# RMSNorms of a two-block transformer kernel: row blocks in pairs, inverse roots by a power on GpSimd

## The chip, the cores and the metric

The kernel runs on one core of a Trainium2 chip. The core has a matmul engine (TensorE, PE in the profile), VectorE (DVE), ScalarE (ACT), GpSimd (POOL) and SyncE (SP, which here only issues transfers). Times are device microseconds (us) of one execution; the time of a kernel is the median of its runs.

## The reference

The input is a sequence of 512 tokens of width 1024. A first block mixes a gated delta rule (4 heads, chunks of 64, both directions, with a state that starts from a context of 256 tokens) and a banded attention of 8 heads; its result is added to x. The second block has two layers, each a feed-forward network, a mixer (causal latent attention beside a dilated one), a feed-forward network and a gated embedding. Each of these is wrapped in two norms: its output is normalised before it is added (postnorm), and the sum is normalised for the next one (prenorm).

```python
def rmsnorm(x, g):
    xf = x.astype(jnp.float32)
    y = xf * lax.rsqrt(jnp.mean(xf * xf, axis=-1, keepdims=True) + EPS)
    return (y * g.astype(jnp.float32)).astype(x.dtype)

def swiglu(x, w_gate, w_up, w_down):
    return (jax.nn.silu(x @ w_gate) * (x @ w_up)) @ w_down

# mixer: norms on the latents and on each group of heads
q = (rmsnorm(q_lat, q_norm) @ w_q_up)
kv = (rmsnorm(kv_lat, kv_norm) @ w_kv_up)
merged = jnp.concatenate([rmsnorm(o_mla, grp_gain[:MLA_WIDTH]),
                          rmsnorm(o_dil, grp_gain[MLA_WIDTH:])], axis=-1)
return merged @ w_out
```

All of it is in 32-bit floats.

## The kernel before

Activations lie with the 1024 features on the partitions, as 8 row blocks of 128, and the 512 tokens along the free axis. A matrix product is done in three passes, with each factor split in a high and a low part: ScalarE copies a weight into its high part wH (L78), VectorE subtracts to get wL (L80), or GpSimd does where the caller says `l="g"`; activations are split in the same way into xnH (L101) and xnL (L105). All matmuls of products come from L87.

A norm works on one half of the tokens (256 columns, `HALVES`). `SumSq.add` squares a row block on ScalarE (L156, L159) and adds it on VectorE into one accumulator (L160). `sums` (L133) multiplies the accumulator by a vector of ones, so that PE sums over the partitions: the result is one number for each token, as 128x2. `rsq` makes the inverse root of it on VectorE: scale and add (rq_v, L112), a first guess by integer shifts (L113, L114), three Newton rounds of three operations (L118 to L120), and where the norm has a factor of its own, a multiplication by it (rq_p, L124). `bcast` (L141) spreads the 256 numbers over all partitions by matmuls, into PSUM. Then `postnorm` scales each row block by gain and root (nt, L189), adds it into h (L191) and feeds the new h to the next SumSq; `prenorm` scales h (ny, L171, in `scaled_split`) and splits it. The tiles of these functions come from a pool `np_`: np1 in the first block (two buffers of each), np2 in the second (three).

Four stages follow each other in a layer: `ffn`, `mixer`, `ffn`, `ple`. The last products of a stage give its output one row block and half at a time, and the first products of the next stage wait for xnH and xnL of a half. In `mixer`, `group` is the norm over the four row blocks of a head group (om, od), and the latents have norms over two row blocks and one.

The first block ends with the delta-rule steps (`gdn_steps`, six steps of eight chains, 4 heads in two directions: a read of the state L598, a product with an inverse L605, the update L617, the output L628 and L629, whose temporaries are tiles gr_, vd and u) and window attention (`win_heads`: K, Q, V and a mask are loaded into a pool "wina", then scores psg<-wK,wQ, a masked softmax wS, transposes L1013, values L1021). The output of the delta rule is squared, normalised (osq) and transposed (L909).

Two things that the source does not spell out set the order. A scheduling layer places the instructions of each engine when the program is built, from the order of the code, the dependences and its own idea of durations. And pools lie on two stacks in SBUF, one from the left and one from the right; where a new tile takes bytes that an older one held, its first write waits for the last use of the older one.

Of the kernel before, what the change touches and what calls it, by code (L numbers as in the profile page):

```python
# [9 lines left out]
F32 = mybir.dt.float32  # L10
# [3 lines left out]
ALU = mybir.AluOpType  # L14
# [12 lines left out]
class Kern:  # L27
    def __init__(self, tc, ctx, I, O):
        self.tc, self.nc, self.I, self.O = tc, tc.nc, I, O
        self.n = 0  # L30
# [10 lines left out]
        nc.vector.memset(self.ones2, 1.0)  # L41

# [65 lines left out]
    def rsq(self, src, n, mul, add, post=None):  # L108

        nc, t = self.nc, lambda nm, dt=F32: self.np_.tile([128, 24], dt, name=nm, bufs=2)[:, :n]  # L110
        v, i, j = t("rq_v"), t("rq_i", I32), t("rq_j", I32)
# [33 lines left out]
    class SumSq:  # L145
        def __init__(self, K):
            self.K, self.a, self.n = K, [None, None], 0

        def add(self, src, scale=1.0):
            K, nc = self.K, self.K.nc  # L150
            p, n = src.shape[0], src.shape[-1]
            i = 0
            self.n += 1
# [12 lines left out]

    def scaled_split(self, H, L, src, gain, rsB, h="a", l="v"):

        n = src.shape[-1]
        y = self.np_.tile([128, 256], F32, name="ny", bufs=self.nb)[:, :n]  # L170
        self.nc.vector.scalar_tensor_tensor(y, src, gain, rsB, op0=ALU.mult, op1=ALU.mult)  # L171
        self.split(H, L, y, h, l)

    def prenorm(self, ss, c, gain):

        rsB = ss.rs(D, (c[1] - c[0]) // 128)
        for k in range(8):
            self.scaled_split(self.xnH[:, k, c[0]:c[1]], self.xnL[:, k, c[0]:c[1]], self.h[:, k, c[0]:c[1]],
                              gain[:, k:k + 1], rsB)

    def postnorm(self, ss, c, f, gain, post=None, out=None):
# [3 lines left out]
        s2 = self.SumSq(self) if out is None else None  # L185
        for k in range(8):
            t = self.np_.tile([128, 256], F32, name="nt", bufs=self.nb)[:, :c[1] - c[0]]
            hk = self.h[:, k, c[0]:c[1]]
            nc.vector.scalar_tensor_tensor(t, f[:, k, c[0]:c[1]], gain[:, k:k + 1], rsB, op0=ALU.mult, op1=ALU.mult)  # L189
# [3 lines left out]
            else:  # L193
                nc.vector.tensor_tensor(t, hk, t, op=ALU.add)
                nc.sync.dma_start(out[:, k, c[0]:c[1]], t)
# [649 lines left out]
    def merge_(self, ctx, wctx, hctx, heads):  # L845
# [94 lines left out]
        ss = [self.SumSq(self) for _ in HALVES]  # L940
# [95 lines left out]
    def ffn(self, l, j, g_out, g_next):  # L1036
# [3 lines left out]
        with ExitStack() as ctx:  # L1040
# [21 lines left out]
            ss = [self.SumSq(self) for _ in HALVES]  # L1062

            def down(W, part, dm, c):
# [14 lines left out]
                if part == len(PARTS) - 1:  # L1079
                    ss[0 if c[0] == 0 else 1].add(fk)  # L1080
# [103 lines left out]
    def mixer(self, l, G):  # L1184
# [8 lines left out]
        with ExitStack() as ctx:  # L1193
# [49 lines left out]
            with ExitStack() as c2:  # L1243
# [10 lines left out]
                for c in HALVES:  # L1254
                    n = c[1] - c[0]
                    sq, sk = self.SumSq(self), self.SumSq(self)
# [11 lines left out]
                    for z in range(3):  # L1268
                        self.scaled_split(latH[:, z, c[0]:c[1]], latL[:, z, c[0]:c[1]], lat[:, z, c[0]:c[1]], qn[:, z:z + 1],
                                          rq if z < 2 else rk)  # L1270
# [38 lines left out]
            def group(o, k0, halves=HALVES):  # L1309
                for c in halves:  # L1310
                    ss = self.SumSq(self)
                    for k in range(4):
                        ss.add(o[:, k, c[0]:c[1]])
                    rsB = ss.rs(512, 2)
                    for k in range(4):
# [389 lines left out]
```

## Time and profile before

| | |
|---|---|
| median of three runs | 3129.61 us (3122.44 to 3131.08) |
| profiled execution | 3144.24 us, of it 3142.3 us span |
| granted PE clock, mean | 0.944 of full speed |
| busy: PE, DVE, ACT, POOL | 2853.6, 1747.3, 1085.4, 344.7 us |

The span is the time from the first to the last instruction on the record. PE's busy share of 91% is an average: the first block has pauses in which PE waits for transfers, and the second has short ones around its norms. A wait belongs to the instruction that came last; the table of waits groups them by the waiting line and by what ended the wait.

### The profile page before, as it was taken

The page shows a single profiled execution, that of the slowest core. Times are in us where ns is not written, and L with a number is a line of the kernel's source. Part 1 is how long each engine was busy: PE and PEld are TensorE (multiplying, and loading weights), DVE is VectorE, ACT ScalarE, POOL GpSimd, SP SyncE. Part 2 cuts the span into 40 slices and gives each one's busy share as a digit, 9 for nine tenths or more (in the row PEclk, how much of TensorE's full clock was granted, in tenths as well). Part 3 has the DMA queues.
Part 4 walks back from the last instruction along what each step waited for, and adds up shares of the span by engine and source line. Part 5 has one row for each costly group of instructions (what it writes and reads, how often), then busy time and mean ns, then how long its engine had stood idle before and what let it go on. Part 6 is the DMA issues. An engine that isn't in the chain of part 4 may idle for free.

```text
span 3142.3 us, 41998 instructions
## 1 busy us (share of the span) xinstructions
PE 2853.6 (91%) x16048; PEld 2392.3 (76%) x16048; DVE 1747.3 (56%) x3733; ACT 1085.4 (35%) x2062; POOL 344.7 (11%) x199
## 2 busy tenths in 40 slices
PE   7999699999999997887999988999989787999987
PEld 2877588678888885667888878888887566888877
DVE  6678907666333475468523378423376457723357
ACT  3443225443222233563322234322233464322223
POOL 3023211422000011002000022000011001000010
PEclk8999769999999998998999998999999898999998
DMA  5325341443222136542222221322234643222321
GB/s 198 98 94 173 91 125 46 146 141 102 100 88 99 59 116 219 149 137 91 94 94 97 91 94 54 111 95 97 88 83 166 178 144 118 95 94 88 100 74 54
DMA packets 151584, 344.29 MB, mean 110 GB/s; under 512 B 37616, under 2 KB 58480, under 8 KB 150872
## 3 DMA queue, kind: packets, MB, share of 16 engines
q1 hardware_dynamic: 142168, 318.55, 31.9%
q10 hardware_dynamic: 9216, 23.07, 2.1%
q8 instruction: 126, 2.06, 0.3%
q14 instruction: 74, 0.61, 0.1%
HBM read 292.02 MB, written 49.54 MB: 109 GB/s over the span
## 4 chain that ended last, share of the span: by engine, by line
PE 71%; DVE 15%; ACT 4%; DMA 4%; issue 3%; POOL 2%; SPq 0%; ACTq 0%; DVEq 0%; POOLq 0%
PE psg L87 31%; PE psx L87 27%; PE psn L87 2%; PE psx L1172 2%; DVE ss L160 2%; DVE big L512 1%; ACT wH L78 1%; DMA wraw<-in_wo 1%; PE psn L141 1%; DVE wL L80 1%; ACT S L1147 1%; DMA wraw<-in_wvd 1%; DVE h L191 1%; DVE cy L386 1%; DVE xnL L105 1%
## 5 line engine op out<-in xcount | busy, mean ns | idle before, releaser
L78 ACT ACTIVATE wH<-wraw 128x1024 fp32r<-128x1024 f32 (+2 forms) x445 | 445.1, 1002 | 1149.7 <-PE psg L87 564.8
L80 DVE TENSOR_TENSOR wL<-wraw,wH 128x1024 fp32r<-128x1024 f32 (+3 forms) x353 | 406.4, 1153 | 458.9 <-ACT wH L78 458.2
L87 PE MATMUL psg<-xnH,wH 128*128 128x512 f32 (+3 forms) x1528 | 549.2, 361 | 11.8 <-ACT xnH L101 6.4
L87 PE MATMUL psg<-xnL,wH 128*128 128x512 f32 (+3 forms) x1528 | 548.9, 360 | 8.8 <-DVE xnL L105 8.8
L87 PE MATMUL psg<-xnH,wL 128*128 128x512 f32 (+3 forms) x1528 | 549.3, 360 | 4.4 <-POOL wL L80 4.4
L80 POOL TENSOR_TENSOR wL<-wraw,wH 128x1024 fp32r<-128x1024 f32 x92 | 224.9, 2451 | 2139.6 <-ACT wH L78 927.2
L87 PE MATMUL psx<-xnH,wL 128*128 128x512 f32 (+1 forms) x1120 | 391.2, 349 | 1.6 <-POOL wL L80 1.6
L87 PE MATMUL psx<-xnH,wH 128*128 128x512 f32 (+1 forms) x1120 | 392.1, 350 | 0.1
L87 PE MATMUL psx<-xnL,wH 128*128 128x512 f32 (+1 forms) x1120 | 392.0, 350 | 0.0
L87 PEld LDWEIGHTS psg<-xnH,wH 128*128 128x128 f32 (+2 forms) x1528 | 297.3, 195 | 52.8 <-ACT xnH L101 8.0
L87 PEld LDWEIGHTS psg<-xnL,wH 128*128 128x128 f32 (+2 forms) x1528 | 297.7, 195 | 49.9 <-DVE xnL L105 11.4
L87 PEld LDWEIGHTS psg<-xnH,wL 128*128 128x128 f32 (+2 forms) x1528 | 297.9, 195 | 45.3 <-POOL wL L80 5.3
L87 PEld LDWEIGHTS psx<-xnH,wL 128*128 128x128 f32 x1120 | 217.1, 194 | 28.4 <-POOL wL L80 1.9
L87 PEld LDWEIGHTS psx<-xnH,wH 128*128 128x128 f32 x1120 | 217.7, 194 | 26.9 <-ACT wH L78 0.3
L87 PEld LDWEIGHTS psx<-xnL,wH 128*128 128x128 f32 x1120 | 217.2, 194 | 25.8
L1056 DVE TENSOR_TENSOR fa<-fs,psx 128x512 f32<-128x512 f32 (+1 forms) x104 | 62.9, 605 | 270.0 <-PE psx L87 268.9
L87 PE MATMUL psg<-aH,wH 128*128 128x512 f32 (+1 forms) x464 | 159.2, 343 | 0.0
L87 PE MATMUL psx<-aL,wH 128*128 128x512 f32 (+1 forms) x464 | 158.8, 342 | 0.0
L87 PE MATMUL psg<-aL,wH 128*128 128x512 f32 (+1 forms) x464 | 158.5, 342 | 0.0
L87 PE MATMUL psx<-aH,wL 128*128 128x512 f32 (+1 forms) x464 | 158.4, 341 | 0.0
L87 PE MATMUL psx<-aH,wH 128*128 128x512 f32 (+1 forms) x464 | 158.4, 341 | 0.0
L87 PE MATMUL psg<-aH,wL 128*128 128x512 f32 (+1 forms) x464 | 158.3, 341 | 0.0
(568 smaller groups left out, 4756.1 us busy)
## 6 DMA issues: line engine op xcount, KB each, us to landing
wraw<-in_gu SPq DMA_DIRECT2D x176, 512.0 KB
wraw<-in_dn SPq DMA_DIRECT2D x64, 448.0 KB
wraw<-in_dn SPq DMA_DIRECT2D x32, 512.0 KB
wraw<-in_wmod SPq DMA_DIRECT2D x24, 512.0 KB
wraw<-in_wrest ACTq DMA_DIRECT2D x24, 512.0 KB
wraw<-in_wo SPq DMA_DIRECT2D x24, 512.0 KB
wraw<-in_win SPq DMA_DIRECT2D x22, 512.0 KB
kh<-KD SPq DMA_DIRECT2D x64, 128.0 KB
```

The lines of the kernel that those rows point to most:

```text
L78: nc.scalar.activation(H[:, :n], raw[:, :n], AF.Copy)
L80: e.tensor_tensor(L[:, :n], raw[:, :n], H[:, :n].bitcast(F32), op=ALU.subtract)
L87: self.nc.tensor.matmul(ps, lhsT=l, rhs=r, start=start and i == 0, stop=stop and i == m - 1)
L105: e.tensor_tensor(L, src, H.bitcast(F32), op=ALU.subtract)
L141: self.nc.tensor.matmul(ps[:, 128 * c:128 * c + 128], lhsT=rs[:, c:c + 1].to_broadcast([128, 128]), rhs=self.ident, start=True, stop=True)
L160: nc.vector.tensor_tensor(self.a[i], self.a[i], q, op=ALU.add)
L191: nc.vector.tensor_tensor(hk, hk, t, op=ALU.add)
L386: nc.vector.scalar_tensor_tensor(y, cb[:, o + j:o + j + n], cw[:, j:j + 1], y, op0=ALU.mult, op1=ALU.add)
L512: nc.vector.tensor_tensor(tm, A[:112, i:i + 1, i + 1:].to_broadcast([112, n, n]), A[:112, i + 1:, i + 1:].rearrange("q j c -> q c j"), op= ...
L1056: nc.vector.tensor_tensor(a, s, pu[:, :n], op=ALU.mult)
L1147: nc.scalar.activation(S, S, AF.Exp, bias=mn[:, i:i + 1], scale=-1.0, accum_out=den[:, i:i + 1])
L1172: nc.tensor.matmul(pv[:, 128 * j:], lhsT=V[:, j, v:v + 64], rhs=R[b][:, o0:o0 + n], start=z == 0 and y == 0, stop=z == 3 and y == 2)
```

## The change

In the second block (`self.pw` set), `rsq` becomes one VectorE operation and one GpSimd power with the exponent -0.5, read from a constant tile `mhalf`; the factor of a postnorm goes into the scale (a factor p on the root is 1/p^2 under it). In the first block Newton's rounds stay, under a new name. SumSq takes two row blocks at a time: squares, additions, and an accumulator that is two blocks wide, so that `sums` has twice the matmuls. The split of a normalised block and the addition into h go by pairs as well; the scaling by gain and root stays one by one, since each row block has its own gain. The mixer's second half copies its output into f on ScalarE and squares it from there, where before VectorE copied and ScalarE squared out of PSUM. The program's last output goes out in four transfers a half, of two row blocks each, instead of eight.

```diff
@@ class Kern
+        self.mhalf = self.const.tile([128, 24], F32, name="mhalf")
+        nc.vector.memset(self.mhalf, -0.5)
...
     def rsq(self, src, n, mul, add, post=None):
+        if not self.pw:
+            return self.newton(src, n, mul, add, post)
+        v, y = t("rq_v"), t("rq_y")
+        z = 1.0 if post is None else 1.0 / (post * post)
+        nc.vector.tensor_scalar(v, src, mul * z, add * z, op0=ALU.mult, op1=ALU.add)
+        nc.gpsimd.tensor_tensor(y, v, self.mhalf[:, :n], op=ALU.pow)
+        return y, v
...
     class SumSq:
-            if self.a[i] is None:
-                self.a[i] = K.np_.tile([128, 256], F32, name="ss_%d" % i, bufs=K.nb - i)[:p, :n]
-                nc.scalar.activation(self.a[i], src, AF.Square, scale=scale)
+            q = K.np_.tile([128, 2, 256], F32, name="sq2", bufs=4)[:p, :m, :w]
+            nc.scalar.activation(q, src, AF.Square, scale=scale)
+            first, self.i = self.i == 0, self.i + m
+            if first:
+                self.a = q
             else:
-                q = K.np_.tile([128, 256], F32, name="ss_q", bufs=K.nb)[:p, :n]
-                nc.scalar.activation(q, src, AF.Square, scale=scale)
-                nc.vector.tensor_tensor(self.a[i], self.a[i], q, op=ALU.add)
+                nc.vector.tensor_tensor(self.a, self.a, q, op=ALU.add)
...
         def rs(self, dim, nch, post=None, eps=EPS):
-            y, _ = K.rsq(K.sums([a for a in self.a if a is not None], nch), nch, 1.0 / dim, eps, post)
+            s = K.sums([self.a[:, x] for x in range(self.a.shape[1])], nch)
+            y, _ = K.rsq(s, nch, 1.0 / dim, eps, post)
...
     def scaled_split(self, H, L, src, gain, rsB, h="a", l="v"):
-        y = self.np_.tile([128, 256], F32, name="ny", bufs=self.nb)[:, :n]
-        self.nc.vector.scalar_tensor_tensor(y, src, gain, rsB, op0=ALU.mult, op1=ALU.mult)
-        self.split(H, L, y, h, l)
+        for k in range(0, src.shape[1], 2):
+            m = min(2, src.shape[1] - k)
+            y = self.np_.tile([128, 2, 256], F32, name="ny2", bufs=2)[:, :m, :n]
+            for x in range(m):
+                self.nc.vector.scalar_tensor_tensor(y[:, x], src[:, k + x], gain[:, k + x:k + x + 1], rsB, op0=ALU.mult, op1=ALU.mult)
+            self.split(H[:, k:k + m], L[:, k:k + m], y, h, l)
...
     def postnorm(self, ss, c, f, gain, post=None, out=None):
-        for k in range(8):
-            t = self.np_.tile([128, 256], F32, name="nt", bufs=self.nb)[:, :c[1] - c[0]]
-            hk = self.h[:, k, c[0]:c[1]]
-            nc.vector.scalar_tensor_tensor(t, f[:, k, c[0]:c[1]], gain[:, k:k + 1], rsB, op0=ALU.mult, op1=ALU.mult)
+        for k in range(0, 8, 2):
+            t = self.np_.tile([128, 2, 256], F32, name="ny2", bufs=2)
+            hk = self.h[:, k:k + 2, c[0]:c[1]]
+            for x in range(2):
+                nc.vector.scalar_tensor_tensor(t[:, x], f[:, k + x, c[0]:c[1]], gain[:, k + x:k + x + 1], rsB, op0=ALU.mult, op1=ALU.mult)
...
     mixer
-                        nc.vector.tensor_copy(fk, ps)
-                        ss.add(ps)
+                        nc.scalar.activation(fk, ps, AF.Copy)
+                    if dm % 2:
+                        ss.add(f[:, dm - 1:dm + 1, c[0]:c[1]])
...
     run
-        self.np_, self.nb = self.pool(ctx, "np2", 1), 3
+        self.np_, self.nb, self.pw = self.pool(ctx, "np2", 1), 3, True
```

The built order moves at three places. The first is PE in the delta-rule steps of the first block. Before, in the step whose update is L617 and whose output is L628 and L629, the scores of window attention (psg<-wK,wQ) stand among them (S is a chain's state, kT, qhat and qk its keys and queries, vd and u the two copies of its values):

```order
L617 MATMUL psx<-vd,kT_3010 128x128 x2
L617 MATMUL psx<-vd,kT_3014 128x128
L87 MATMUL psg<-wK,wQ 128x256
L617 MATMUL psx<-vd,kT_3014 128x128
L87 MATMUL psg<-wK,wQ 128x256
L617 MATMUL psx<-vd,kT_3018 128x128
L87 MATMUL psg<-wK,wQ 128x256
L617 MATMUL psx<-vd,kT_3018 128x128
L628 MATMUL psx<-S_3152,qhat 128x128
L629 MATMUL psx<-u,qk 128x128
L628 MATMUL psx<-S_3156,qhat 128x128
```

After (line numbers are some 19 higher there: the output is L647 and L648, the transposes of its squares L928, products L89), the end of the last step and what follows:

```order
L647 MATMUL psx<-S_3590,qhat 128x128
L648 MATMUL psx<-u,qk 128x128
L647 MATMUL psx<-S_3594,qhat 128x128
L648 MATMUL psx<-u,qk 128x128
L647 MATMUL psx<-S_3598,qhat 128x128
L648 MATMUL psx<-u,qk 128x128
L928 MATMUL psx<-ident,osq 128x128 x12
L89 MATMUL psg<-wK,wQ 128x256 x8
L89 MATMUL psg<-wK,wQ 128x128 x2
L89 MATMUL psg<-wK,wQ 128x256 x4
L89 MATMUL psg<-wK,wQ 128x128 x2
```

All scores have moved behind the last step and behind twelve transposes of osq; no row of wK and wQ stands earlier.

The second place is PE in the first layer, where the first half of the second feed-forward network's output is summed for its postnorm (L133 and L141 before, L145 and L153 after, ss and sq2 the accumulators). Before, from the sum on (the broadcast of rq_p comes 23 rows after the sum):

```order
L87 MATMUL psg<-aH,wL 128x256
L133 MATMUL psn<-ones_68,ss_15728 128x2 x2
L87 MATMUL psg<-aH,wH 128x256
L87 MATMUL psg<-aL,wH 128x256
L87 MATMUL psg<-aH,wL 128x256
L87 MATMUL psg<-aH,wH 128x256
L87 MATMUL psg<-aL,wH 128x256
L87 MATMUL psg<-aH,wL 128x256
L87 MATMUL psg<-aH,wH 128x256
L87 MATMUL psg<-aL,wH 128x256
```

After:

```order
L89 MATMUL psg<-aH,wH 128x256
L89 MATMUL psg<-aL,wH 128x256
L145 MATMUL psn<-ones_68,sq_15199 128x2 x4
L89 MATMUL psg<-aH,wL 128x256
L89 MATMUL psg<-aH,wH 128x256
L89 MATMUL psg<-aL,wH 128x256
L89 MATMUL psg<-aH,wL 128x256
L153 MATMUL psn<-ident,rq_y 128x128 x2
L89 MATMUL psx<-aH,wH 128x256
```

The sum now has four matmuls of two accumulators, and four products stand between it and the broadcast, where there were 22.

The third place is GpSimd's queue, from the end of the first block (mt) to the middle of the first layer. Before, with wL the weight subtractions, kr and rp_u rotations in the mixer:

```order
L998 TENSOR_TENSOR wS<-wS,wrd 128x512
L938 TENSOR_TENSOR mt<-mt,ra 128x512 x8
L80 TENSOR_TENSOR wL<-wraw,wH 128x1024 x12
L1275 TENSOR_TENSOR kr_9752<-kr_9752,kr_9753 32x512
L1119 TENSOR_TENSOR rp_u<-rp_u,rp_v 128x512 x10
L80 TENSOR_TENSOR wL<-wraw,wH 128x1024 x28
L1275 TENSOR_TENSOR kr_20331<-kr_20331,kr_20332 32x512
L1119 TENSOR_TENSOR rp_u<-rp_u,rp_v 128x512 x10
L80 TENSOR_TENSOR wL<-wraw,wH 128x1024 x16
```

After:

```order
L957 TENSOR_TENSOR mt<-mt,ra 128x512 x8
L82 TENSOR_TENSOR wL<-wraw,wH 128x1024 x8
L118 TENSOR_TENSOR rq_y<-rq_v,mhalf 128x2 x3
L82 TENSOR_TENSOR wL<-wraw,wH 128x1024 x3
L118 TENSOR_TENSOR rq_y<-rq_v,mhalf 128x2
L82 TENSOR_TENSOR wL<-wraw,wH 128x1024
L118 TENSOR_TENSOR rq_y<-rq_v,mhalf 128x2 x2
L1293 TENSOR_TENSOR kr_9566<-kr_9566,kr_9567 32x512
L118 TENSOR_TENSOR rq_y<-rq_v,mhalf 128x2 x2
L1138 TENSOR_TENSOR rp_u<-rp_u,rp_v 128x512 x10
L118 TENSOR_TENSOR rq_y<-rq_v,mhalf 128x2 x5
L82 TENSOR_TENSOR wL<-wraw,wH 128x1024 x3
```

The powers (rq_y<-rq_v,mhalf) stand among the subtractions and rotations, which were in unbroken rows.

## Rows read from the trace of the kernel before

**Rows 1.** The page: busy us of the engines, share of the span, instructions

```profile
PE 2853.6 (91%) x16048; PEld 2392.3 (76%) x16048; DVE 1747.3 (56%) x3733; ACT 1085.4 (35%) x2062; POOL 344.7 (11%) x199
```

**Rows 2.** PE's waits, 700 to 3143: total us, times, longest us

```profile
PE psn L133 <- DVE ss L160: 40.9, 14, 7.7
PE psn L141 <- DVE rq_y L120: 38.3, 21, 5.9
PE psn L141 <- DVE rq_p L124: 12.8, 7, 4.6
...
PE psg L87 <- DVE xnL L105: 8.8, 7, 1.7
```

**Rows 3.** VectorE by line, 700 to 3142: busy us, mean ns, idle before

```profile
L160 DVE TENSOR_TENSOR ss<-ss,ss_q 128x256 f32<-128x256 f32 x248 | 132.6, 540 | 30.9 <-ACT ss_q L159 29.7 <-ACT ss L156 0.3
...
L1056 DVE TENSOR_TENSOR fa<-fs,psx 128x512 f32<-128x512 f32 x72 | 49.5, 688 | 257.7 <-PE psx L87 257.7
...
L112 DVE TENSOR_SCALAR rq_v<-psn 128x2 f32<-128x2 f32 x48 | 7.5, 157 | 22.2 <-PE psn L133 22.1
```

**Rows 4.** The chain of waits, one norm: start us, duration us, what

```profile
1085.11 0.17 DVE rq_v L112
...
1088.70 0.18 DVE rq_p L124
1089.02 0.68 PE psn L141 x4
1089.70 2.37 PE psg L87 x20
```

**Rows 5.** GpSimd by line, whole span

```profile
L80 POOL TENSOR_TENSOR wL<-wraw,wH 128x1024 fp32r<-128x1024 f32 x92 | 224.9, 2451 | 2139.6 <-ACT wH L78 927.2 <-DVE rq_a L118 711.0 <-PE psn L133 373.0
...
L998 POOL TENSOR_TENSOR wS<-wS,wrd 128x640 f32<-128x640 f32 x16 | 20.2, 1283 | 0.0
L998 POOL TENSOR_TENSOR wS<-wS,wrd 128x512 f32<-128x512 f32 x16 | 17.6, 1098 | 19.6 <-ACT wPH L101 18.2 <-DVE wrd L995 1.1
...
L971 POOL MEMSET wden<- 128x8 f32 x8 | 0.8, 105 | 114.2 <-DVE wrd L994 114.1
```

**Rows 6.** Timelines of two norms: start us, duration us, instruction, [idle before]

```profile
1835.39 0.16 DVE L120 SCALAR_TENSOR_TENSOR rq_y<-rq_b,rq_y 128x2 f32<-128x2 f32 x1
...
1835.85 2.35 POOL L80 TENSOR_TENSOR wL<-wraw,wH 128x1024 fp32r<-128x1024 f32 x1 [352.65 <-DVE rq_a L118]
1835.98 2.24 DVE L120 SCALAR_TENSOR_TENSOR rq_y<-rq_b,rq_y 128x2 f32<-128x2 f32 x1
...
1838.57 0.68 PE L141 MATMUL psn<-ident,rq_p 128*128 128x128 f32 x4 [2.29 <-DVE rq_p L124]
...
1850.53 4.83 POOL L80 TENSOR_TENSOR wL<-wraw,wH 128x1024 fp32r<-128x1024 f32 x2 [2.55 <-ACT wH L78]
...
1850.98 2.17 DVE L160 TENSOR_TENSOR ss<-ss,ss_q 128x256 f32<-128x256 f32 x1
```

**Rows 7.** Delta-rule steps: window, length, PE, PEld, DVE, ACT, POOL busy, clock, DMA, GB/s

```profile
483.30:545.50 62.20, 59.69 (x427) 52.96 (x426) 45.61 (x155) 37.23 (x119) 10.58 (x13) 1.00 0.05 14
```

**Rows 8.** PE by line in that stretch

```profile
L87 PE MATMUL psg<-wK,wQ 128*128 128x256 f32 (+1 forms) x64 | 14.6, 316 | 0.2 <-DVE wmn L981 0.2
...
L1013 PE MATMUL psn<-ident,wS 128*128 128x128 f32 x33 | 6.3, 276 | 0.8 <-POOL wS L998 0.8
L1021 PE MATMUL psg<-wPH,wV 128*64 128x512 f32 (+2 forms) x17 | 5.7, 368 | 0.0
L1021 PE MATMUL psg<-wPL,wV 128*64 128x512 f32 (+2 forms) x8 | 3.3, 412 | 0.0
```

**Rows 9.** Same columns, the stretch in which K and mask were loaded

```profile
440.00:480.00 40.00, 38.51 (x269) 31.87 (x269) 4.74 (x17) 12.09 (x28) 2.43 (x3) 0.72 0.52 163
```

**Rows 10.** PE's one long wait, and the stretch after it

```profile
PE psx L551 <- DMA Y<-dX: 24.4, 1, 24.4
...
360.00:420.00 60.00, 57.83 (x464) 45.43 (x465) 35.51 (x33) 17.09 (x28) 10.37 (x4) 0.66 0.36 93
```

More of the change, by code (lines that the diff above doesn't have):

```diff
@@ L184, in postnorm @@
         rsB = ss.rs(D, (c[1] - c[0]) // 128, post)
-        s2 = self.SumSq(self) if out is None else None
-        for k in range(8):
-            t = self.np_.tile([128, 256], F32, name="nt", bufs=self.nb)[:, :c[1] - c[0]]
-            hk = self.h[:, k, c[0]:c[1]]
-            nc.vector.scalar_tensor_tensor(t, f[:, k, c[0]:c[1]], gain[:, k:k + 1], rsB, op0=ALU.mult, op1=ALU.mult)
+        s2 = self.SumSq(self, 8) if out is None else None
+        for k in range(0, 8, 2):
[3 more added lines that the diff above has]
+                nc.vector.scalar_tensor_tensor(t[:, x], f[:, k + x, c[0]:c[1]], gain[:, k + x:k + x + 1], rsB, op0=ALU.mult, op1=ALU.mult)
             if out is None:
@@ L194, in postnorm @@
                 nc.vector.tensor_tensor(t, hk, t, op=ALU.add)
-                nc.sync.dma_start(out[:, k, c[0]:c[1]], t)
+                nc.sync.dma_start(out[:, k:k + 2, c[0]:c[1]], t)
         return s2
@@ L939, in merge_ @@
             self.split(yH[:, dm], yL[:, dm], t)
-        ss = [self.SumSq(self) for _ in HALVES]
+        ss = [self.SumSq(self, 8) for _ in HALVES]
         ws = {}
@@ L1060, in gw @@
                 return [self.w(I["gu"][l, j, ff, z], 8, 128, l=l2[z]) for z in range(2)]
-            ss = [self.SumSq(self) for _ in HALVES]
+            ss = [self.SumSq(self, 8) for _ in HALVES]
             def down(W, part, dm, c):
@@ L1078, in down @@
                     nc.vector.tensor_tensor(fk, fk, ps[:, :n], op=ALU.add)
-                if part == len(PARTS) - 1:
-                    ss[0 if c[0] == 0 else 1].add(fk)
+                if part == len(PARTS) - 1 and dm % 2:
+                    ss[0 if c[0] == 0 else 1].add(f[:, dm - 1:dm + 1, c[0]:c[1]])
             def dw(part, dm):
@@ L1255, in mixer @@
                     n = c[1] - c[0]
[L1256 removed]
+                    sq, sk = self.SumSq(self, 2), self.SumSq(self, 1)
                     for z in range(4):
@@ L1267, in mixer @@
                     rq, rk = sq.rs(256, 2), sk.rs(128, 2)
-                    for z in range(3):
-                        self.scaled_split(latH[:, z, c[0]:c[1]], latL[:, z, c[0]:c[1]], lat[:, z, c[0]:c[1]], qn[:, z:z + 1],
-                                          rq if z < 2 else rk)
+                    for z, r in ((slice(0, 2), rq), (slice(2, 3), rk)):
+                        self.scaled_split(*[x[:, z, c[0]:c[1]] for x in (latH, latL, lat)], qn[:, z], r)
                     for g in range(2):
@@ L1310, in group @@
                 for c in halves:
-                    ss = self.SumSq(self)
-                    for k in range(4):
-                        ss.add(o[:, k, c[0]:c[1]])
+                    ss = self.SumSq(self, 4)
+                    for k in (0, 2):
+                        ss.add(o[:, k:k + 2, c[0]:c[1]])
                     rsB = ss.rs(512, 2)
-                    for k in range(4):
-                        self.scaled_split(self.xnH[:, k0 + k, c[0]:c[1]], self.xnL[:, k0 + k, c[0]:c[1]], o[:, k, c[0]:c[1]],
-                                          gg[:, k0 + k:k0 + k + 1], rsB)
+                    k = slice(k0, k0 + 4)
+                    self.scaled_split(self.xnH[:, k, c[0]:c[1]], self.xnL[:, k, c[0]:c[1]], o[:, :, c[0]:c[1]], gg[:, k], rsB)
             po = self.pool(ctx, "heads", 1)
@@ L1407, in mixer @@
             for c in HALVES:
-                ss = self.SumSq(self)
+                ss = self.SumSq(self, 8)
                 for dm in range(8):
@@ L1436, in ple @@
             for c in HALVES:
-                ss = self.SumSq(self)
+                ss = self.SumSq(self, 8)
                 for dm in range(8):
@@ L1498, in second @@
         nc, I = self.nc, self.I
-        G = lambda l: [self.gains[:, l, i] for i in range(8)]
+        G = lambda l: [self.gains[:, l, i, :] for i in range(8)]
         for l in range(2):
@@ L1532, in run @@
             for c in HALVES:
-                ss = self.SumSq(self)
-                for k in range(8):
-                    ss.add(self.h[:, k, c[0]:c[1]])
+                ss = self.SumSq(self, 8)
+                for k in range(0, 8, 2):
+                    ss.add(self.h[:, k:k + 2, c[0]:c[1]])
                 self.prenorm(ss, c, self.gains[:, 0, 0])
```

23 lines of the change are left out of this document (13 added, 10 removed).

## The prediction

> **What bounds the kernel now.** I read the engine totals first: TensorE (PE) is busy 2853.6 us, 91% of the span [rows 1], so the kernel is bound by matmuls and only PE's idle stretches can be won. The idle list of PE over the second block (700 to 3143 us) says what ended each of them: 40.9 us for the last add of a sum of squares (L160, in 14 waits), 38.3 and 12.8 us for the inverse root (L120 and L124), 8.8 us for the low part of a normalised block (L105) [rows 2]. The 51.1 us on the inverse root are what the change is aimed at. The last view is a table by stage of the first block: from 483.3 to 545.5 us PE is busy 59.7 of 62.2 us at full clock [rows 7], with two jobs interleaved, the delta-rule steps and window attention. That stretch is not what the change is about, but the change reaches it.
>
> The profiled execution took 3144.2 us against a median of 3129.6, so I sum changes on 3144.2 and scale by 3129.6/3144.2 = 0.9954.
>
> **Inverse root, second block.** There are 48 (L112 x48 [rows 3]). In a quiet one rq_v starts at 1085.11, rq_p at 1088.70 for 0.18 us, and the broadcast L141 at 1089.02 [rows 4]: 3.9 us from sums to broadcast, 0.14 us of it a handover to PE. Now there is one VectorE operation (0.17), one pow on GpSimd (d), and a second handover, which I price as the first: 0.17 + 0.14 + d + 0.14 = 0.45 + d. No row shows a pow or a two-column two-input operation of GpSimd. The nearest rows: a MEMSET 128x8 takes 0.105 us, products of 512 and 640 columns 1.098 and 1.283 us [rows 5]. The line through the last two has 1.45 ns a column and leaves 0.36 us at two columns. Bounds for d: 0.1 to 1.1 us. I take 0.45, the line's end with a little for the power itself.
>
> What PE does meanwhile is set by the new order: before, 20 to 45 matmuls mostly stand between a sum and its broadcast, now 4 to 7. At 2.37/20 = 0.118 us each [rows 4] these cover 0.6 us, where before they covered 2.4 to 5.3. So the cover is spent with the saving. A stall is 0.45 + d - 0.6 = d - 0.15 in some 38 norms, and 0.45 + d in about 5 without cover (the two dilated group norms of a layer now stand back to back, and the last norm of all). With d = 0.45: 38 x 0.3 + 5 x 0.9 = 16 us.
>
> The pow also stands in GpSimd's one queue. Before, it ran the second block's weight subtractions (wL, L80, 2.45 us each [rows 5]) in rows of 12, 28 and 16. Now pows stand among them, so that a pow behind a running wL waits up to 2.45 us, with the broadcast and then all normalised blocks behind it. About 24 norms lie in such stretches; I let six of them meet the middle of a wL, 6 x 1.2 = 7 us. Together 23 us against 51: **-28 us**. Ends: d = 0.1 with no queue gives about 3 us (-48); d = 1.1 gives 38 x 0.95 + 5 x 1.55 = 44, with 15 of queue 59 (+8).
>
> **Port shared by VectorE and GpSimd.** The trace shows a fact that speaks both ways. While GpSimd subtracts a wL from 1835.85 to 1838.20, an rq_y, which at 1835.39 took 0.16 us, lasts 2.24 us, and the broadcast comes 2.29 us late [rows 6]. At 1850.98 an add of squares lasts 2.17 us, while two wL run [rows 6]. So a Newton chain was exposed at each of its two-input steps, which go.
> The Trainium skill, "SBUF — State Buffer", section "Who interferes with whom", gives the rule: a VectorE instruction with two SBUF inputs and a GpSimd instruction that reads SBUF exclude each other for the whole instruction, whoever starts first. The trace agrees (2.24 against 0.16 us). By the rule a pow is in its turn held up by an add of a pair that is running (up to 0.69 us): if a third of 43 norms met half of one, 5 us more, which my sum leaves out.
>
> **Sums of squares and additions by pairs.** A chain from output to sum had seven adds of 128x256 (0.540 us each with their waits [rows 3]) and eight of h; now three and four of twice the width, priced by 128x512 rows (0.688 [rows 3]). Fewer two-input operations can be caught by a wL: 7 instead of 15 in a half. I put half of the 40.9 us at L133 down to such catches and half of these gone: -10. Against it, the end of the chain is longer: the last add takes 0.69 instead of 0.43 or so, the last square about as much more, and sums of two accumulators need twice the matmuls (0.59 us for a norm's before). That is +0.7 us or more in 14 waits, +10; VectorE's freed time (some 12 small operations of 0.2 us a norm) comes back in the tight ones, -7. Net **-7 us** (-25 to +12). Splits by pairs deliver the first normalised block later, by one more scaling and a wider copy and subtraction; the waits on xnL were 8.8 us in 7 [rows 2], and I add **+4** (0 to +10). The mixer's copy of f goes from VectorE to ScalarE, which is no nearer to a limit: nothing. In the output's tail four transfers replace eight: nothing.
> Second block: -28 - 7 + 4 = **-31 us** (-70 to +25).
>
> **First block: what the larger tiles displace.** There Newton stays, and SumSq's and scaled_split's tiles grow: before ss_0, ss_q and ny at two buffers of 1 KB, now sq2 at four and ny2 at two of 2 KB. That is 6 KB a partition more, in a pool that lies beneath everything else of the block, and mhalf's 96 bytes. The steps' tiles move up into the place where window attention puts its mask, its sink and K. These must now wait until the steps are over. The order shows it: before, the matmuls of wK with wQ stand among the steps; now the steps stand alone, then twelve transposes of osq, then the first wK.
>
> What leaves the stretch: 14.6 us of PE for the scores, 6.3 for L1013, 9.0 for L1021 [rows 8], 30 us of busy time, which by the spacing of pipelined matmuls (52 x 0.15 + 12 x 0.11 + 33 x 0.11 + 25 x 0.25, estimates from their starts) may be only 18. I take 24. The steps alone are a chain of PE, VectorE and ScalarE; they took 62.2 us together with the rest, and PE needs 29 us for them; I take the middle, 46. Then the loads: mask 512 KB, K 4 x 192 KB and a Q of 64 KB are 1.38 MB, at 163 GB/s (the rate of the stretch in which they were loaded before [rows 9]) 8 us with nothing to cover them but the transposes. The scores, masks and softmax then need some 3 us to start. And the clock: after a wait of 24.4 us PE ran at 0.66 from 360 to 420 us [rows 10]; a shorter idle costs less, I say 3 us. From the pauses of 545 to 560 us about 6 us go. Sum: 46 + 24 + 8 + 3 + 3 - 62 - 6 = **+16 us**. Ends: -3 if the steps need 33 us and the moved work 18, +35 if they keep 59 and it takes 30.
>
> **Sum.** -31 + 16 = -15: 3129 in the profile, **3115 us** scaled.
>
> **Rivals.**
> *All cover holds.* d is 0.1 to 0.2, the queue is free when a pow comes, the steps alone are short: -43 - 15 + 4 + 5 = -49, 3081 us. For it: a MEMSET needs 0.105 us; against it: a MEMSET reads nothing, and wL at 2.45 us stand in the queue.
> *The two blocks cancel.* The second gains its 31, the first loses 30 since the steps keep their length and the loads come late: 3129 us. For it: PE was 96% busy in a stretch that held both jobs. Against it: the steps had to share PE with attention.
> *Slower: the handover to GpSimd.* If a pow takes 1.1 us, each of 43 norms stalls PE by 1 to 1.5 us, since the order leaves only 0.6 us of cover: +8 in place of -28, -7 + 4 as before, +16 in the first block: +21, 3151 us; with 30 in the first block 3165. It decides from d where 43 d eats the rest: (51 - 3.5 - 43 d) + 7 - 4 - 16 = 0 gives d = 0.8 us. For it: the shortest two-input operation of GpSimd in these rows takes 1.098 us [rows 5]. Against it: it has 512 columns.
> The Trainium skill, "GPSIMD Engine Reference", section "Instruction dispatch", says that the first call of freshly loaded code there costs some 6 us; no row here shows one. By it one pow, the first, would add 6 us to each case; my sum stands without it.
>
> **Chances.** Forecast (3096 to 3124) 0.40, cover holds (under 3096) 0.18, cancel (3124 to 3142) 0.22, slower 0.20. The range 3076 to 3150 leaves out the far ends of the second and the last. A measurement of this kernel tells 0.3% (9.4 us) from no change; so faster (under 3120) is 0.36 + 0.18 = 0.54, within 0.3% (to 3139) 0.23, slower 0.23. The likeliest case alone: 3096 to 3124.
>
> **What would show it.** In the new profile the GpSimd row of L118 (rq_y from rq_v and mhalf) gives d; idle time of PE ended by it should be near 23 us in all, and that ended by the add of squares 34. wL and pow should alternate on GpSimd with a few pows over 1 us late. In the first block the first scores should come after the last delta-rule step, with PE idle or at low clock between, and the stretch from 483 us to the second block should be 16 us longer. I am wrong if the steps fill less than 35 or over 60 us, if pow takes over 0.8 us, or if PE's idle time at L133 doesn't change while VectorE's does.

## Result: 0.6% slower, where 0.5% faster was forecast

The changed kernel takes 3154.27 us (median of six runs, 3145.33 to 3158.35), the kernel before 3130.35 us in the same comparison; the ratio is 1.0063 (95% interval 1.0040 to 1.0087). This ratio is an estimate from all runs and not the quotient of the two medians, which is 1.0076; below, differences "by the ratios" are differences of such ratios. The range forecast ended at 3150.

Engine totals of the changed kernel (busy us, share, instructions; against [rows 1] PE has 22 us more, VectorE 147 us less):

```profile
PE 2876.0 (91%) x16200; PEld 2407.1 (76%) x16200; DVE 1600.7 (51%) x2916; ACT 1056.9 (34%) x1858; POOL 391.2 (12%) x245
```

PE's waits in its second block (columns as in [rows 2]; psn, psg and psx are tiles in PSUM that PE writes, wraw a weight as it was loaded):

```profile
PE psn L145 <- DVE sq L174: 47.6, 16, 4.9
PE psg L89 <- DMA kh<-KD: 29.4, 2, 15.4
PE psx L89 <- ACT wH L80: 25.3, 3, 10.6
PE psn L153 <- POOL rq_y L118: 24.0, 32, 2.1
```

The wait for the root fell from 51.1 us to 24.0, as forecast. The wait for the add of squares rose from 40.9 to 47.6 (34 was forecast), those on xnL are gone from the list, and there is a wait for weights, wH, of 25.3 us in three; in the kernel before no wait for wH in this stretch is longer than 1.1 us.

Where the time is, by stage (window, length, busy PE, PEld, DVE, ACT, POOL, clock, DMA, GB/s). The cuts are the first product of the delta-rule steps with a state, and the first sum of the norm that ends the first block. Before:

```profile
0.00:474.70 474.70, 415.50 (x2384) 316.90 (x2385) 308.31 (x607) 170.86 (x300) 113.50 (x67) 0.87 0.41 130
474.70:715.30 240.60, 221.89 (x1263) 175.45 (x1262) 161.97 (x383) 112.85 (x278) 64.90 (x54) 0.97 0.33 106
715.30:3142.30 2427.00, 2216.25 (x12404) 1899.98 (x12403) 1277.00 (x2744) 801.73 (x1484) 166.34 (x78) 0.96 0.33 106
```

Changed:

```profile
0.00:462.00 462.00, 406.29 (x2385) 307.81 (x2385) 311.07 (x608) 170.59 (x300) 114.71 (x67) 0.90 0.42 130
462.00:726.80 264.80, 233.58 (x1263) 180.97 (x1261) 159.95 (x383) 113.49 (x278) 65.06 (x54) 0.94 0.32 101
726.80:3151.60 2424.80, 2236.08 (x12555) 1918.32 (x12555) 1129.66 (x1926) 772.83 (x1280) 211.41 (x124) 0.96 0.33 106
```

The first rows hold the same work: before, its profiled execution ran there at a clock of 0.87 against 0.90 and lost 12.7 us that the change has no part in (that execution was 14 us above its median). The second rows are 24.2 us longer with the change. In the third, PE's idle time fell from 210.8 to 188.7 us (length less busy), but its busy time rose by 19.8, which leaves 2.2 us of gain.

Most of the added busy time is the sums. The same line in both kernels, from the second block (busy us, mean ns, idle before), first before, then changed:

```profile
L133 PE MATMUL psn<-ones,ss 128*128 128x2 f32 x184 | 28.1, 257 | 41.2 <-DVE ss L160 40.9
```

```profile
L145 PE MATMUL psn<-ones,sq 128*128 128x2 f32 x336 | 50.8, 271 | 47.0 <-DVE sq L174 46.8
```

By these rows 152 more records of two columns are 22.7 us, 0.149 us each, where one of 256 columns takes 0.118 us [rows 4]. (A sum stands in the trace as two records for one instruction: the built order has four of them in a changed norm, the trace eight. A product stands as one.) One norm of the changed kernel (timeline) shows both prices, eight records of sums in 1.02 us and the root in 0.98 us from rq_v to the broadcast:

```profile
1847.07 1.02 PE L145 MATMUL psn<-ones,sq 128*128 128x2 f32 x8
1848.21 0.16 DVE L117 TENSOR_SCALAR rq_v<-psn 128x2 f32<-128x2 f32 x1 [1.28 <-PE psn L145]
1848.44 0.69 POOL L118 TENSOR_TENSOR rq_y<-rq_v,mhalf 128x2 f32<-128x2 f32 x1 [339.83 <-DVE rq_v L117]
1849.19 0.71 PE L153 MATMUL psn<-ident,rq_y 128*128 128x128 f32 x4 [0.51 <-POOL rq_y L118]
```

GpSimd's row of the power (by line, busy us and mean ns behind the bar), and its durations (ns, least, median and longest):

```profile
L118 POOL TENSOR_TENSOR rq_y<-rq_v,mhalf 128x2 f32<-128x2 f32 x46 | 39.4, 857 | 1877.0 <-DVE rq_v L117 1856.4 <-PE psg L89 18.4 <-PE psx L89 2.1
```

```profile
L118 POOL TENSOR_TENSOR rq_y<-rq_v,mhalf x46: 688/689/1669, 1107.7 to 3139.1; 128x2 f32<-128x2 f32 x46
```

A power takes 0.69 us, in the mean 0.86. The excess is 8 us over the 46. Ten powers, of 1.08 to 1.67 us, hold 7.4 us of it. Each of the ten started while VectorE was in an operation with two inputs in SBUF (a subtraction wL or an add of squares), and ended 0.55 to 0.56 us after that operation. One of them (timeline):

```profile
1434.67 1.23 DVE L82 TENSOR_TENSOR wL<-wraw,wH 128x1024 fp32r<-128x1024 f32 x1
1434.77 1.67 POOL L118 TENSOR_TENSOR rq_y<-rq_v,mhalf 128x2 f32<-128x2 f32 x1 [42.81 <-DVE rq_v L117]
```

That is what the rule of the Trainium skill on the shared port ("SBUF — State Buffer", "Who interferes with whom") says of a GpSimd operation that comes second. The other way round did not show: two adds of squares that started 0.01 and 0.06 us after a power took 0.72 and 0.69 us, where the median of that line is 0.69. The 6 us that the Trainium skill ("GPSIMD Engine Reference", "Instruction dispatch") has for the first call of freshly loaded code did not show either: the first power started 0.08 us after its rq_v had ended and took 0.71 us.

In the first block all scores come after the last step, as the order said. PE's longest wait there is for osq, not for K; the mask and K go out only when the steps end, at 523.3, and the first scores start at 534.92 (timeline, the columns start and duration first):

```profile
523.74 0.37 SPq L832 DMA_DIRECT2D wmk<-in_k_wmask  x1
524.63 1.81 SPq L844 DMA_DIRECT2D wK<-KW  x4
...
531.07 3.01 PE L928 MATMUL psx<-ident,osq 128*128 128x128 f32 x12 [7.80 <-DVE osq L924]
534.92 1.40 PE L89 MATMUL psg<-wK,wQ 128*128 128x256 f32 x5 [0.84 <-DMA wQ<-QW]
```

The stretch of [rows 7] begins at the first product of the second step with a state. From the same product on, the changed kernel has these three stages, to the end of the steps, to the first scores and to the second block (table of stages):

```profile
470.60:523.30 52.70, 48.78 (x305) 40.05 (x304) 30.84 (x103) 21.52 (x74) 1.04 (x1) 1.00 0.00 1
523.30:534.90 11.60, 3.01 (x12) 2.15 (x13) 7.96 (x25) 0.63 (x1) 3.56 (x3) 0.57 0.74 193
534.90:726.80 191.90, 173.92 (x897) 132.31 (x897) 116.22 (x240) 88.73 (x195) 60.46 (x50) 0.95 0.40 127
```

The kernel before, behind the stretch of [rows 7]:

```profile
545.50:715.30 169.80, 154.33 (x788) 116.04 (x787) 111.38 (x212) 73.01 (x152) 54.32 (x42) 0.96 0.43 140
```

The steps alone take 52.7 us, 9.5 less than together with attention; then come 11.6 us to the first scores; the rest takes 22.1 us more. Together that is the 24.2 us. The 122 matmuls that left the steps took only 10.9 us of PE's busy time with them (59.7 to 48.8).

And at 744 us PE waits 10.6 us for a weight (timeline):

```profile
750.36 2.97 SPq L70 DMA_DIRECT2D wraw<-in_gu  x2
753.88 2.01 ACT L80 ACTIVATE wH<-wraw 128x1024 fp32r<-128x1024 f32 x2 [3.33 <-DMA wraw<-in_gu]
754.99 0.58 PE L89 MATMUL psx<-xnH,wH 128*128 128x256 f32 x1 [10.64 <-ACT wH L80]
```

What SyncE's queue waited for from 700 to 760 us, in which that transfer stands:

```profile
SPq L70 <- POOL wL L82: 36.8, 4, 29.2
SPq L70 <- DVE xnL L107: 12.6, 1, 12.6
SPq L70 <- DVE sq L174: 11.9, 1, 11.9
```

Without Newton's tiles the second block's norm pool ends 1.3 KB lower, and the weight buffers above it begin at byte 54912 of a partition in the built program; the first block's norm pool, grown by 6 KB, ends at 56064. (The tile sizes give the same difference: 12,672 bytes for sq2, ny2, rq_v and rq_y in the second pool, 13,824 in the first, where Newton has eight small tiles.) So the first weight load had to wait for the last norm of the first block to have read its tile, and SyncE's queue is in order.

### The profile page after: what moved, and what is told of

Same layout as the page of the kernel before. It is cut to its first block, busy times and chain, and to the rows that moved or that the text cites. A ratio compares the mean times of both kernels' runs of the same rounds, so it can differ in the third digit from the quotient of the medians.

```text
span 3151.6 us, 41200 instructions
## 1 busy us (share of the span) xinstructions
PE 2876.0 (91%) x16200; PEld 2407.1 (76%) x16200; DVE 1600.7 (51%) x2916; ACT 1056.9 (34%) x1858; POOL 391.2 (12%) x245
## 5 line engine op out<-in xcount | busy, mean ns | idle before, releaser
L89 PE MATMUL psg<-xnH,wL 128*128 128x512 f32 (+3 forms) x1528 | 547.0, 358 | 1.9 <-POOL wL L82 1.9
L89 PE MATMUL psg<-xnH,wH 128*128 128x512 f32 (+3 forms) x1528 | 546.9, 358 | 1.7 <-ACT xnH L103 1.7
L89 PE MATMUL psg<-xnL,wH 128*128 128x512 f32 (+3 forms) x1528 | 546.2, 357 | 0.0
L89 PE MATMUL psx<-xnH,wH 128*128 128x512 f32 (+1 forms) x1120 | 391.7, 350 | 10.6 <-ACT wH L80 10.6
L89 PE MATMUL psx<-xnH,wL 128*128 128x512 f32 (+1 forms) x1120 | 390.7, 349 | 1.2 <-POOL wL L82 1.2
L89 PE MATMUL psx<-xnL,wH 128*128 128x512 f32 (+1 forms) x1120 | 390.0, 348 | 0.0
L89 PEld LDWEIGHTS psg<-xnH,wL 128*128 128x128 f32 (+2 forms) x1528 | 293.8, 192 | 43.3 <-POOL wL L82 2.1
L89 PEld LDWEIGHTS psg<-xnH,wH 128*128 128x128 f32 (+2 forms) x1528 | 293.6, 192 | 41.9 <-ACT xnH L103 2.1
L89 PEld LDWEIGHTS psg<-xnL,wH 128*128 128x128 f32 (+2 forms) x1528 | 293.5, 192 | 41.6 <-DVE xnL L107 1.1
L118 POOL TENSOR_TENSOR rq_y<-rq_v,mhalf 128x2 f32<-128x2 f32 x46 | 39.4, 857 | 1877.0 <-DVE rq_v L117 1856.4
L82 POOL TENSOR_TENSOR wL<-wraw,wH 128x1024 fp32r<-128x1024 f32 x92 | 232.0, 2528 | 286.7 <-ACT wH L80 280.3
L89 PEld LDWEIGHTS psx<-xnH,wH 128*128 128x128 f32 x1120 | 216.2, 193 | 38.0 <-ACT wH L80 10.9
L89 PEld LDWEIGHTS psx<-xnH,wL 128*128 128x128 f32 x1120 | 215.1, 192 | 29.2 <-POOL wL L82 1.5
L89 PEld LDWEIGHTS psx<-xnL,wH 128*128 128x128 f32 x1120 | 215.3, 192 | 27.4
L89 PE MATMUL psg<-aH,wL 128*128 128x512 f32 (+1 forms) x464 | 159.5, 344 | 0.0
L89 PE MATMUL psx<-aH,wH 128*128 128x512 f32 (+1 forms) x464 | 159.0, 343 | 0.0
L89 PE MATMUL psg<-aH,wH 128*128 128x512 f32 (+1 forms) x464 | 158.8, 342 | 0.1
L89 PE MATMUL psx<-aH,wL 128*128 128x512 f32 (+1 forms) x464 | 158.7, 342 | 0.0
L89 PE MATMUL psg<-aL,wH 128*128 128x512 f32 (+1 forms) x464 | 158.7, 342 | 0.0
```

The lines of the kernel that those rows point to most:

```text
L82: e.tensor_tensor(L[:, :n], raw[:, :n], H[:, :n].bitcast(F32), op=ALU.subtract)
L89: self.nc.tensor.matmul(ps, lhsT=l, rhs=r, start=start and i == 0, stop=stop and i == m - 1)
L118: nc.gpsimd.tensor_tensor(y, v, self.mhalf[:, :n], op=ALU.pow)
```

## Experiments

All times are medians, and ratios are to the kernel before in the same session (medians of 3127.1 to 3130.4 us), with their 95% interval. The last column has PE's idle and busy time from the first sum at the first block's end on, by the table of stages; it is of one profiled execution, which need not lie at the median.

| kernel | us | ratio | idle, busy us |
|---|---|---|---|
| before | 3130.4 | 1 | 211, 2216 |
| changed | 3154.3 | 1.0063 (1.0040 to 1.0087) | 189, 2236 |
| e1 before, first block displaced | 3148.3 | 1.0069 (1.0052 to 1.0086) | 205, 2216 |
| e2 changed, weight buffers clear | 3143.4 | 1.0044 (1.0026 to 1.0062) | 180, 2232 |
| e3 changed, first block's norms old | 3125.6 | 0.9992 (0.9975 to 1.0008) | 178, 2241 |
| e4 changed, accumulator folded | 3135.6 | 1.0027 (1.0008 to 1.0047) | 184, 2224 |
| e5 before, with the power | 3147.1 | 1.0060 (1.0036 to 1.0084) | 210, 2236 |
| e6 changed, with Newton | 3139.5 | 1.0038 (1.0023 to 1.0053) | 175, 2233 |
| e7 e3 and e4 together | 3105.2 | 0.9932 (0.9916 to 0.9949) | 175, 2226 |
| e8 e3, squares by single blocks | 3130.6 | 1.0002 (0.9984 to 1.0020) | 206, 2214 |
| e9 e7 with Newton | 3137.2 | 1.0027 (1.0011 to 1.0042) | 210, 2222 |
| e10 changed, tables late | 3143.2 | 1.0041 (1.0022 to 1.0060) | 180, 2242 |
| e11 e9, tables late | 3132.3 | 1.0008 (0.9987 to 1.0028) | 211, 2217 |
| e12 e7, tables late | 3105.1 | 0.9932 (0.9906 to 0.9958) | 174, 2217 |

**The first block.** e1 leaves before as it is but for an unused tile:

```diff
             self.np_, self.nb = self.pool(c1, "np1", 1), 2
+            pad = self.np_.tile([128, 1560], F32, name="pad")
+            nc.vector.memset(pad[:, :2], 0.0)
```

> The kernel before with nothing changed but an unused tile of 6,240 bytes a partition in the first block's norm pool, so that all above it moves up as in the changed kernel. Theory A (the larger tiles cost the first block its overlap of delta-rule steps and window attention): 20 to 26 us slower than before, PE idle some 8 us after the last step. Rival B (the first block's loss in the profile is the granted clock of one execution, and the loss lies in the norms): within 5 us of before.

Its stretch of the first block (table of stages) is as long as the changed kernel's, 263.6 against 264.8 us:

```profile
459.70:723.30 263.60, 231.33 (x1263) 178.67 (x1261) 159.48 (x383) 113.56 (x278) 65.11 (x54) 0.96 0.33 103
```

PE waits 7.8 us for osq behind the last step there too. The tile alone makes the kernel 0.69% slower: theory A, and the whole loss of the change by itself.

e2 widens the root's tiles of the second block, which lifts the weight buffers above the first block's norm pool:

```diff
-        v, y = t("rq_v"), t("rq_y")
+        v, y = [self.np_.tile([128, 104], F32, name=nm, bufs=2)[:, :n] for nm in ("rq_v", "rq_y")]
```

> The changed kernel with 1,280 bytes more in the second block's root tiles, so that the second set of weight buffers begins above the first block's norm tiles, as in the kernel before. If the 10.6 us wait for wH at 744 us comes from the weight load that waits for those tiles: 8 to 10 us faster than the changed kernel (13 to 16 us slower than before), and the wait gone. If it comes from the row of weights in ScalarE's queue, no change.

SyncE's waits from 700 to 760 us no longer name xnL, and of PE's three waits for wH (25.3 us) two are left:

```profile
SPq L70 <- POOL wL L82: 50.4, 8, 28.7
SPq L70 <- DVE sq L174: 12.5, 1, 12.5
```

```profile
PE psx L89 <- ACT wH L80: 14.1, 2, 7.1
```

By the ratios this is worth 0.19%, 6 us, a little under what was expected. The two intervals overlap, so the time alone does not show the gain; the trace shows that the wait is gone and where it came from.

e3 gives the first block's one user of SumSq and prenorm the code of before (one block at a time, `SumSq1`, `prenorm1`):

```diff
-        ss = [self.SumSq(self, 8) for _ in HALVES]
+        ss = [self.SumSq1(self) for _ in HALVES]
...
-            self.prenorm(ss[z], c, self.gains[:, 0, 0])
+            self.prenorm1(ss[z], c, self.gains[:, 0, 0])
```

> The changed kernel with the first block's norms in their old form and size (single row blocks, 6 KB); the second block as changed. Theory A: the displacement and the late weight load both go, 24 + 9 = 33 us faster than the changed kernel, some 10 us faster than before. Rival B: as slow as the changed kernel.

```profile
460.80:703.30 242.50, 222.90 (x1264) 176.44 (x1262) 161.93 (x383) 113.06 (x278) 64.87 (x54) 0.96 0.33 105
703.30:3122.30 2419.00, 2240.61 (x12555) 1922.19 (x12555) 1141.63 (x1934) 773.18 (x1288) 212.48 (x124) 0.96 0.33 106
```

The first block is back at 242.5 us (240.6 before), and idle time at 178. Of the 33 us expected 22 came by the ratios, where e1 and e2 measured 22 and 6 us for the two parts; with intervals of some 5 us to either side these agree. (In the profiles PE was busy 9 us longer in its second block than in e2, with the same matmuls, x12555 in both; but e2's profiled execution was 6 us under its median.)

**The sums.** e4 adds the halves of the accumulator first:

```diff
-            s = K.sums([self.a[:, x] for x in range(self.a.shape[1])], nch)
+            a = self.a[:, 0]
+            if self.a.shape[1] == 2:
+                K.nc.vector.tensor_tensor(a, a, self.a[:, 1], op=ALU.add)
+            s = K.sums([a], nch)
```

> The changed kernel with the two halves of the accumulator added on VectorE (one 128x256 addition) ahead of the sums, so that a norm has four matmuls for its sums instead of eight. Theory C (the second block keeps only a third of its gain because the sums' extra matmuls load the engine that bounds the kernel): PE busy 20 us less, 12 to 20 us faster than the changed kernel. Rival D (PE has idle time at those places anyway, so the sums cost nothing and the added addition costs 0.4 us a norm): 0 to 10 us slower than the changed kernel.

e7 has this and e3's edit:

> The changed kernel with the first block's norms in their old form and, in the second block, the two halves of the accumulator added on VectorE ahead of the sums. If the two costs found add up: 3126 - 12 = 3114 us, some 14 us faster than before.

PE's sums in e7 (line) are near those of before, 31.8 us against 28.1, and PE's waits did not grow for the added operation:

```profile
L145 PE MATMUL psn<-ones,sq 128*128 128x2 f32 x184 | 31.8, 277 | 43.6 <-DVE sq L210 43.1
```

```profile
PE psn L145 <- DVE sq L210: 43.1, 16, 4.8
PE psn L153 <- POOL rq_y L118: 16.8, 26, 2.0
```

Theory C, with a little less than it said: 0.36% by the ratios in e4 (11 us, the intervals just overlap), 0.6% from e3 to e7 (19 us). PE's busy time in its second block fell by 12 us in e4 and by 14.5 in e7, and not by the 20 expected, though the 152 records are gone in both; its idle time fell by 4 to 5. So the sums' rows, 22.7 us, say more than removing them gives back: the times of neighbouring matmuls overlap. e7 came out 9 us faster than expected, which is not explained. With e12 below it is the fastest that was found, 0.68% faster than before.

**What the power is worth.** e5 puts only the power (rsq of the change, with mhalf and pw) into the kernel before:

> The kernel before with the inverse root of the second block by the one power on GpSimd, and nothing by pairs. Theory C (the power is worth its 27 us of waits, the pairs' sums took them back): waits at L141's counterpart fall from 51 to some 24 us, the sums stay at 22 us of PE, 18 to 27 us faster than before. Rival E (the order spends the shorter root on shorter cover, so nothing is won): within 6 us of before.

```profile
PE psn L141 <- DVE ss L168: 61.4, 20, 6.1
PE psn L149 <- POOL rq_y L117: 26.3, 30, 3.3
PE psx L89 <- ACT wH L80: 11.1, 2, 5.9
PE psx L89 <- POOL wL L82: 7.8, 3, 4.9
```

Neither theory: slower by 0.6%. (L141 is the sum here, L149 the broadcast.) The broadcast's waits halved, 51.1 to 26.3, but the sums' rose from 40.9 to 61.4, and PE waits 11.1 us for weights wH at the start of the mixers, as it does in the changed kernel and not in the kernel before; idle time is unchanged (210 and 211 us). For the first part of this the built order says why: in the twenty norms at the stage boundaries after the heads, 520 matmuls stood between sums and broadcasts before, 105 in e5 (102 in the changed kernel, 91 in e7). The work that can cover a norm is given; a shorter root lets the scheduler place it elsewhere. The 20 us more of busy time go with a lower clock (0.95 against 0.96 in the row of the stage), but the profiled execution is the slowest of e5's six, 3161.1 us at a granted clock of 0.941. Over all executions the mean clock is that of the kernel before, 0.947 and 0.946, and e5 is still 0.6% slower: where a middling execution loses its 19 us is not shown.

e6 is the changed kernel with Newton, pw never set:

> The changed kernel with Newton's rounds in the second block too; pairs as changed. Its weight buffers lie clear of the first block's norm tiles, so it is to be compared with the changed kernel with 1,280 bytes more (3143 us). Theory C: 15 to 27 us slower than that. Rival E: within 6 us of it.

As fast as e2 (0.06% faster by the ratios), so rival E: with pairs and eight sums the power is worth nothing. PE's waits in e6, and then in e2, which has the power:

```profile
PE psn L145 <- DVE sq L174: 30.3, 15, 4.7
PE psn L153 <- DVE rq_y L132: 26.1, 16, 5.9
PE psn L153 <- DVE rq_p L136: 13.2, 8, 4.5
```

```profile
PE psn L145 <- DVE sq L174: 48.4, 16, 4.8
PE psn L153 <- POOL rq_y L118: 22.6, 30, 2.1
```

The power takes some 17 us off the broadcast's waits and puts 18 us on the sums'. Beside that e2 has the 14.1 us of wH shown above; e6 has none that is longer than 0.4 us. So a part of what the power costs is the order of the weight loads that comes with it.

e9 is e7 with Newton:

> The fastest version so far (first block's norms old, accumulator folded on VectorE, pairs elsewhere, 3105 us) with Newton's rounds in place of the power. If the power is worth nothing once the norms go by pairs: within 6 us of it. If the power earns the waits at the broadcast that it takes away: 12 to 25 us slower than it.

0.95% slower than e7, 30 us. Here the power earns its waits:

```profile
PE psn L153 <- DVE rq_y L132: 36.9, 22, 5.5
PE psn L145 <- DVE sq L210: 36.5, 12, 4.7
PE psn L153 <- DVE rq_p L136: 18.3, 10, 4.6
```

55.2 us wait for the root, 36.5 for the sum, where e7 has 16.8 and 43.1. So the power is worth -19 us (e5), nothing (e6) or 30 us (e9), as the rest of the norm, and the built order with it, stands; why the folded version leaves Newton's root exposed and the unfolded e6 does not (39 us at the broadcast) is not settled.

e8 takes squares and their additions block by block in e3, with the power and the other pairs kept:

```diff
-            q = K.np_.tile([128, 2, 256], F32, name="sq2", bufs=4)[:p, :m, :w]
-            nc.scalar.activation(q, src, AF.Square, scale=scale)
...
+            for x in ([src] if len(src.shape) == 2 else [src[:, k] for k in range(src.shape[1])]):
...
+                    nc.scalar.activation(q, x, AF.Square, scale=scale)
+                    nc.vector.tensor_tensor(self.a, self.a, q, op=ALU.add)
```

> The changed kernel with the first block's norms in their old form and squares and sums of single row blocks in the second block; the power, the splits and the additions into h by pairs stay. PE's sums at 22 us. If pairs in the squares are worth VectorE's freed time: some 3 us slower than the one with the folded accumulator; if their longer last link costs more than that: 3 to 8 us faster than it, 17 to 25 us faster than before.

A miss: 0.7% slower than e7, 22 us. PE waits for the last add in 21 places:

```profile
PE psn L145 <- DVE ss L203: 66.9, 21, 6.7
```

So squares by pairs are worth 24 us of waits at the sums, 66.9 against 43.1, once their sums are folded.

**The weights behind the tables.** e10 writes the loads of the mixer's masks and rotation tables (mk and tab) behind its weight loads wv:

> The changed kernel with the transfers of the mixer's masks and rotation tables written behind its weight loads; by the built order 1 MB of tables now goes out behind three of the four wvd weights (it went ahead of all). If PE's waits for wH at 1140 and 2340 us (7.6 and 7.0 us) come from these transfers: the two waits halved, 4 to 9 us faster than the changed kernel. If they come from the weight buffers' release: no change.

```profile
PE psx L89 <- ACT wH L80: 10.4, 1, 10.4
```

The one wait left is that at the start of the second block; the two at 1140 and 2340 us went, 0.22% by the ratios (7 us, again with intervals that overlap). The same edit in e9 (e11) and in e7 (e12), whose orders already had a weight ahead of the tables:

> As the version with Newton's rounds, old first block and folded accumulator, and masks and tables behind all four wvd weights. If the transfers' order is worth 4 to 9 us: that much faster than the one without; else within 3 us.

> The fastest version so far (3105 us, with the power) with the mixer's masks and tables written behind its weight loads; one wvd weight goes out ahead of them, as in the version without the edit, so at most 3 us either way from the 0.5 us that the tables' place changes.

e11 is 0.19% faster than e9, with intervals that overlap; e12 is as fast as e7, though e7's two waits for wH (8.9 us) are gone from its list and PE's idle time is the same (174 and 175 us). So a wait for weights that is taken away need not shorten the kernel.

## Why the prediction was wrong

Two steps failed, one in each block, and one cost stood nowhere in the sum. The stages put numbers on it: the second block was to gain 31 us and gained 2.2; the first was to lose 16 and lost 24.2.

**Sums of squares by pairs (-7 us): the step that failed in the second block.** "Sums of two accumulators need twice the matmuls" was priced only in the 14 waits, within +10. They are work of the engine that bounds the kernel, in all 46 norms: PE is busy 19.8 us longer in the block, of which the line's rows show 22.7 before overlap, and with the sums folded 12 to 14.5 us of busy time and 11 to 19 us of the kernel come back. The locks that I let go (-10) did not go: 16 adds of squares took over 1 us before and 18 after (counted in the timelines), and the waits at the sums rose by 6.7 us.

**First block (+16 us): the displacement right, the length of the steps wrong.** e1 and e3 show the displacement from both sides, 23 us in the table of stages and 22 by the ratios. "PE needs 29 us for them; I take the middle, 46" is what failed: alone, the steps keep PE busy for 48.8 us and take 52.7, from the same product on as the 62.2 before. The other terms held. To the first scores it took 11.6 us, against 8 + 3. The wait in it ends with osq, behind a reduction and a Newton chain, but wQ lands only 0.84 us after the transposes that follow, so that the loads alone would have held the scores nearly as long (this was not tried). The moved work, with the pauses and the clock, came to 22.1 us, against 24 + 3 - 6. (Two slips in the working change nothing: the spacings add up to 19 us and not 18, and the ends of the second block to -73 and +30 in place of -70 and +25.)

**Not in the sum at all.** PE waits 25.3 us for wH. 10.6 us is the weight load that waits for the first block's norm tiles (e2), 14.6 us in two waits are the weights queued behind the tables (e10). Removed one by one they are worth 6 and 7 us by the ratios, neither clear of noise. I had followed what the larger np1 pushes up, not what the smaller np2 pulls down.

**Inverse root, second block (-28 us): right as a wait, open as a gain.** The waits fell by 27.1 us, to 24.0 where 23 was the sum. That close a hit is in part luck: with the measured 0.69 us for the power in place of 0.45 the same sum gives 33, and the chain from rq_v to the broadcast was shorter than the two handovers in it, 0.98 us in place of 1.14. The working also took the cover between sum and broadcast to be spent and left out that those 49 us of products (418 by 0.118 us) then stand before the sums or behind the broadcast; it counted one end of a moved wait. In e5, with the power alone, the sums' waits rise by 20.5 us and idle time is the same.

**Splits by pairs (+4 us).** The waits on xnL, 8.8 us, left the list; with the same splits they are 6.0 us in e4 and e7, so the sign of this term is not settled.

The rival "cancel" has the first block nearer, 30 us, but from steps that keep their length, which they did not; its second block is wrong as the forecast's is. The slower rival's 3151 us lies next to the 3154 measured, but by luck: its power takes 1.1 us and stalls every norm, and at 0.69 us the power is below its own point of decision, 0.8 us. None of the three signs of being wrong came (steps under 35 or over 60 us, a power over 0.8, idle time at the sums unchanged): they watched the terms in the sum, and the loss lay mostly beside them.

The mixer's copy on ScalarE and the four transfers of the output, both priced at nothing, were not tried by themselves.

## What to carry to other kernels

Count every instruction that a change adds to the engine that bounds the kernel, in all places and not only where it waits; a matmul of few columns is not a cheap one. When tiles change size, list what begins and ends beside them on the pool's stack on both sides, and look for a load in an in-order queue that now waits for an old tile. Where a scheduler fills the gaps, a shorter chain moves its filling: look at the sum of idle time over a boundary, not at one wait.

## What was not expected of the hardware

A record of a sum's 128x2 takes 0.128 us of PE (8 in 1.02 us), more than one of a 128x256 product at 0.118 us [rows 4], and a sum has two records where a product has one. Against a broadcast's 128x128, which also has two records for an instruction and takes 0.17 us each (4 in 0.68 us [rows 4]), 64 times fewer columns save a quarter.

A power of two columns on GpSimd takes 0.69 us, where the line through 512 and 640 columns [rows 5] gives 0.36 us and a MEMSET 0.105 us; what another two-input operation of two columns takes is not shown. A power that starts during a VectorE operation with two inputs in SBUF is held until that operation ends, up to 1.67 us in all.
